# Global attention in a hybrid attention / recurrence / ConvFFN layer: second scores keys-first, values and ones stationary, probabilities streaming

## The chip, the cores and the metric

The kernel runs on one core of one Trainium2 chip. The metric is device time in microseconds (us) of one execution; the time of a kernel is the median of its runs. A core has the engines that the profile calls PE (TensorE, matrix products; PEld is its loading of the stationary operand), DVE (VectorE), ACT (ScalarE), POOL (GpSimd) and SP (SyncE, which here issues the DMAs). Each works through its own list of instructions in order and waits for others by semaphores. In a matrix product one operand is stationary (up to 128 x 128) and the other streams through it column by column into a bank of PSUM; a tile in SBUF or PSUM has 128 partitions.

## What is computed

One layer on 1024 latent tokens of width 1024 and 256 context tokens: a modulated RMSNorm, a projection, three mixers, a gated merge, and a ConvFFN. The change touches the second mixer, `yb`, attention over 1280 keys, 256 of the context and 1024 latent ones, with 8 query heads that share 2 key/value heads of 64 channels:

```python
def dense_attn(q, k, v, sink=None):
    ...
    s = jnp.einsum('bqkgd,bjkd->bkgqj', q.reshape(B_, Lq, KV, G, hd), k).astype(jnp.float32) * hd ** -0.5
    p = jax.nn.softmax(s, axis=-1)[..., :k.shape[1]].astype(v.dtype)
    return jnp.einsum('bkgqj,bjkd->bqkgd', p, v).reshape(B_, Lq, HQ * hd)

def global_attn(q, k, v, ck, cv):
    k_all = jnp.concatenate([ck, k], axis=1)
    v_all = jnp.concatenate([cv, v], axis=1)
    ...

...
ya = window_attn(aq, ak, av, cak, cav, sink_a[l])
yb = global_attn(bq, bk, bv, cbk, cbv)
x_mix = x + m_lat[:, :, 2] * merge_branches(ya, yb, yc, gates, w_branch[l], w_out[l])
```

`dense_attn` is called for each block of 128 queries. In `merge_branches` each mixer's output is lifted to width 1024, multiplied by its sigmoid gate (a part of the projection), summed, and multiplied by `w_out`.

## The kernel before

**Numbers in two halves.** Inputs are fp32. For most products a number is split into a high half, which is the number rounded to fp32r (a cast on ACT), and a low half, which is what remains (a subtraction on DVE). A product is then three matmuls: high by high, high by low, low by high (L190 to L211). Weights come as 512 KB loads `wr` and are split into `wh` and `wl` in `w_unit` (L175, L176). Ordinary transposes on PE are products with an identity matrix, `ident` in fp32 or `identr` in fp32r.

**Stages.** The program computes norms and projections, then the recurrence, then the token-major parts of the projection (L597), then the two attentions in a loop over `br` (L629: 0 is the window attention, 1 the global one), then the merge (L1453) and the ConvFFN. Queries, keys and values lie in DRAM between stages (`q_d`, `kv_d`), and so do the gates (`gate_d`) and the mixers' outputs (`y_d`).

**Order of the work.** The tile framework puts the instructions of each engine into one fixed order when the kernel is built, close to the order in which the program names them, with some priorities (L1322). `weave` (L1214) interleaves generators by their step counts: in each attention the scores of iteration `it + 1`, the values of iteration `it`, and a filler, the products of the gates (`gate_unit` L507: 24 matmuls into one bank for half a unit, tile `gz`, then a copy `gs` on ACT and a store). The window attention has 7 units of gates as filler and the global one 7; 32 filler steps are woven into the lead of each, `FILL0`. PSUM has three tags: `mm`, two tiles of two banks; `a`, two banks; `b`, two banks. A tile of a tag waits until the tile that held its bank is read.

**Global attention.** 16 iterations: 8 blocks of 128 queries, for each of 2 key/value heads (`g`), with its 4 query heads. The lead loads keys and values in five pieces of 256 keys (`prep`, L1247): a load `kv` in a buffer of tag `qf`, `VHL` with the high and low half of the values side by side, 64 columns each, the high halves of the keys twice and the low halves twice (`kk`), their fp32r transposes `kt` in bank `a`, and copies into `KH` and `KL`, which hold 64 channels twice on 128 partitions. The queries (`qprep`, L1273) are split into high and low, which share the 128 partitions of `QT`, so that one product with `KH` gives high times (high and low), and one with `KL` adds low times both.

The scores (`softmax_global`, L1411) are query-first: a tile has 128 queries on the partitions and keys in the columns, 256 context keys of the four heads in `sbc`, 1024 keys of one head in `sbl`, each by a product with `KH` and one with `KL`. DVE takes the largest of each row, ACT the exponential with that bias and the row's sum in the same instruction (`pc`, `plat`); the reciprocals are spread by POOL (L1446) and turned on PE (`pr`, L1314).

The values (L1297) need the keys on the partitions: for each of 10 key tiles, four fp32 transposes turn the probabilities of the four heads into `pp` (L1319, bank `a`), ACT casts the high half `ph` (L1323), DVE subtracts the low half `pl` (L1324), and two tiles later (`PV_LAG`) two products add them into `po` (L1305, L1306, bank `b`), with `VHL` stationary and the 512 columns of 4 heads by 128 queries streaming. At the end the two halves of `po` are added, multiplied by the turned reciprocals, and stored (L1335 to L1342).

## Time and profile before

| | us |
|---|---|
| median of 3 runs (range) | 2117.54 (2116.04 to 2120.67) |
| the profiled execution, its own time | 2119.41 |
| its span, from the first to the last instruction | 2117.6 |

The span by stage, from the view of the profile that sums busy time by windows (us):

| window | stage | PE | DVE | ACT | POOL |
|---|---|---|---|---|---|
| 0 to 700 | norms, projections, recurrence | 680.71 | 413.17 | 206.39 | 57.27 |
| 700 to 880 | window attention | 175.68 | 145.09 | 139.75 | 49.83 |
| 880 to 1210 | global attention | 326.95 | 255.40 | 267.85 | 6.44 |
| 1210 to 1300 | begin of the merge | 89.87 | 49.60 | 31.86 | 0.00 |
| 1300 to 2117 | merge, ConvFFN | 805.13 | 516.14 | 357.12 | 176.14 |

How such a profile is read: the page gives each engine's busy time, the span in forty slices with tenths of busy time in each, and groups of instructions by line with count, busy time, the mean duration of one and the idle time of the engine ahead of them with what ended it. `out<-in` are the program's tile names. The trace gives the same by windows of time and as a timeline of single instructions. A matmul's duration runs from its start to a modelled end; matmuls overlap, so that the pace of PE is read from the distance between starts. In a window's row the engines stand as busy us with the count of instructions, then the clock granted to PE as a share of full speed, the share of the DMA engines, and GB/s. In a timeline's row, `SPq` is the queue of SP, whose instructions issue DMAs.

### The profile page before, as it was taken

What the parts mean: (1) busy time and instruction counts of PE and PEld (TensorE: products, weight loads), DVE (VectorE), ACT (ScalarE), POOL (GpSimd) and SP (SyncE); (2) the same over time, 40 slices, a digit from 0 to 9 for tenths busy, and PEclk for the clock granted to TensorE, in tenths of its full rate; (3) what the DMA queues carried; (4) which work ended last, traced back from release to release, by engine and by line L of the source; (5) the groups of instructions that cost most, each with busy time, mean ns of one, the idle gap of its engine ahead of it and who ended that gap; (6) DMA issues with size and microseconds to landing.
All of it is one profiled execution on the core that took longest, in us unless ns stands there. A gap on an engine that the chain in (4) does not pass through costs nothing.

```text
span 2117.6 us, 30402 instructions
## 1 busy us (share of the span) xinstructions
PE 2078.3 (98%) x11622; PEld 1735.2 (82%) x11622; DVE 1379.4 (65%) x2299; ACT 1003.0 (47%) x1760; POOL 289.7 (14%) x257
## 2 busy tenths in 40 slices
PE   7999999999999999999999999999999999999997
PEld 4888888888988788888888788888888888888887
DVE  4736756636565788677887747569777777664423
ACT  4333323311122877688888734346444444453322
POOL 0000000010022222100000000011333344100111
PEclk9999999999999999999999999999999999999999
DMA  9511111136644221211110454541322222295332
GB/s 364 205 44 36 46 50 32 50 113 201 195 139 134 85 60 53 81 45 33 36 33 28 133 188 147 192 151 49 100 86 84 90 71 89 80 304 192 108 124 85
DMA packets 95489, 229.66 MB, mean 108 GB/s; under 512 B 10736, under 2 KB 35696, under 8 KB 94320
## 3 DMA queue, kind: packets, MB, share of 16 engines
q1 hardware_dynamic: 95344, 227.72, 32.4%
q8 instruction: 91, 1.49, 0.3%
q14 instruction: 54, 0.44, 0.1%
HBM read 182.07 MB, written 45.61 MB: 108 GB/s over the span
## 4 chain that ended last, share of the span: by engine, by line
PE 69%; DVE 3%; ACT 2%; issue 1%; POOL 1%; DMA 1%; DVEq 0%; ACTq 0%; POOLq 0%; SPq 0%
PE pp L1319 5%; PE gz L199 3%; PE gz L200 3%; PE gz L201 3%; PE dn L929 3%; PE dn L930 3%; PE dn L928 3%; PE up L852 2%; PE up L853 2%; PE up L854 2%; PE po L1305 2%; PE po L1306 2%; PE br L200 2%; PE br L201 2%; PE br L199 2%; PE upc L854 2%
## 5 line engine op out<-in xcount | busy, mean ns | idle before, releaser
L175 ACT CAST wh<-wr 128x1024 fp32r<-128x1024 f32 (+1 forms) x139 | 145.1, 1045 | 397.7 <-PE dn L929 71.8
L176 DVE TENSOR_TENSOR wl<-wr,wh 128x1024 fp32r<-128x1024 f32 (+1 forms) x139 | 171.2, 1232 | 226.5 <-ACT wh L175 217.4
L1324 DVE TENSOR_TENSOR pl<-pp,ph 128x512 fp32r<-128x512 f32 x236 | 159.5, 688 | 30.4 <-ACT ph L1323 25.0
L199 PE MATMUL gz<-hh,wh 128*128 128x512 f32 x384 | 156.7, 409 | 2.8 <-ACT gs L523 2.8
L200 PE MATMUL gz<-hl,wh 128*128 128x512 f32 x384 | 152.8, 398 | 0.0
L201 PE MATMUL gz<-hh,wl 128*128 128x512 f32 x384 | 152.6, 398 | 0.0
L1323 ACT CAST ph<-pp 128x512 fp32r<-128x512 f32 x236 | 135.7, 585 | 33.6 <-PE pp L1319 31.1
L210 PE MATMUL tm<-wl,hh 128*128 128x256 f32 x384 | 109.0, 284 | 3.4 <-DVE wl L176 3.4
L211 PE MATMUL tm<-wh,hl 128*128 128x256 f32 x384 | 108.8, 283 | 0.0
L209 PE MATMUL tm<-wh,hh 128*128 128x256 f32 x384 | 108.8, 283 | 0.0
L1305 PE MATMUL po<-ph,VHL 128*128 128x512 f32 x236 | 106.4, 451 | 1.7 <-ACT ph L1323 1.1
L929 PE MATMUL dn<-ac,wh 128*128 128x512 f32 x256 | 99.7, 390 | 0.0
L930 PE MATMUL dn<-ac,wl 128*128 128x512 f32 x256 | 99.6, 389 | 0.0
L928 PE MATMUL dn<-ac,wh 128*128 128x512 f32 x256 | 99.6, 390 | 0.0
L1306 PE MATMUL po<-pl,VHL 128*128 128x512 f32 x236 | 98.0, 415 | 0.1
L199 PEld LDWEIGHTS gz<-hh,wh 128*128 128x128 f32 x384 | 73.0, 190 | 16.5 <-ACT gs L523 5.0
L201 PEld LDWEIGHTS gz<-hh,wl 128*128 128x128 f32 x384 | 72.9, 190 | 15.2
L200 PEld LDWEIGHTS gz<-hl,wh 128*128 128x128 f32 x384 | 73.2, 191 | 11.5
L210 PEld LDWEIGHTS tm<-wl,hh 128*128 128x128 f32 x384 | 73.7, 192 | 4.4 <-DVE wl L176 4.0
L1319 PE MATMUL pp<-ident,plat 128*128 128x128 f32 x512 | 77.1, 274 | 0.0
L1319 PEld LDWEIGHTS pp<-ident,plat 128*128 128x128 f32 x512 | 63.2, 141 | 17.0 <-DVE pl L1324 1.2
L733 ACT ACTIVATE u<-c,cw 128x1024 f32<-128x1024 f32 x38 | 47.3, 1246 | 61.9 <-DVE c L889 33.1
(1402 smaller groups left out, 5899.8 us busy)
## 6 DMA issues: line engine op xcount, KB each, us to landing
wr<-in_w_cm SPq DMA_DIRECT2D x48, 512.0 KB, 3.7
wr<-in_w_up SPq DMA_DIRECT2D x44, 512.0 KB, 3.6
wr<-in_w_down SPq DMA_DIRECT2D x33, 512.0 KB, 3.6
wmr<-in_w_mod SPq DMA_DIRECT2D x32, 512.0 KB, 4.6
gate_d<-gs SPq DMA_DIRECT2D x48, 256.0 KB, 2.0
sgt<-gate_d SPq DMA_DIRECT2D x24, 512.0 KB, 3.3
act_d<-u SPq DMA_DIRECT2D x22, 512.0 KB, 2.6
st<-act_d SPq DMA_DIRECT2D x44, 256.0 KB, 4.2
```

Of the source, the lines that this page charges most:

```text
L175: A.copy(hi[:, :n], raw[:, :n])
L176: (lo_eng or V).tensor_tensor(out=lo[:, :n], in0=raw[:, :n], in1=hi[:, :n].bitcast(F32), op=ALU.subtract)
L199: T.matmul(psl, wh[:, k, c], hh[:, k0 + k, cols], start=s, stop=False)
L200: T.matmul(psl, wh[:, k, c], hl[:, k0 + k, cols], start=False, stop=False)
L201: T.matmul(psl, wl[:, k, c], hh[:, k0 + k, cols], start=False, stop=e)
L210: T.matmul(psl, hh[:, k, toks], wl[:, k % 4, :], start=False, stop=False)
L928: T.matmul(z, w[0][:, c], h[0], start=s, stop=False)
L929: T.matmul(z, w[0][:, c], h[1], start=False, stop=False)
L930: T.matmul(z, w[1][:, c], h[0], start=False, stop=e)
L1305: T.matmul(po, vv, ph, start=n == 0, stop=False)
L1319: T.transpose(pp[:, h], PT(h, n), ident)
L1324: V.tensor_tensor(out=pl, in0=pp, in1=ph.bitcast(F32), op=ALU.subtract)
```

## The change

Only the global attention changes, `attention_t` for `br` 1; the window attention keeps `attention`, with the branches for the global one taken out.

- *Stationary values.* `VV[0]` holds for each key tile and head pair high values, 64 columns of ones, high values; `VV[1]` low values, zeros, low values. Of a stationary block of 128 columns, half is values and half ones (or zeros), so that one product gives the values' sum in 64 rows of `po` and the probabilities' sum in the other 64.
- *Maxima first* (`maxima`). The query-first scores are made with `KH` alone. DVE takes the largest of each row; its negative is written in high and low halves into two columns of `QM`, beside the high half of the queries (which POOL copies there), and turned into `M`.
- *Keys-first scores* (`values`). For each pair of key tiles, four products: `KH` stationary with the turned queries `Q`, and `KL`, which has two rows of ones now, with `M`, so that low keys times high queries and the negative maximum are added in one. ACT takes the exponential `e` of 128 keys by 1024 columns. The cast `ph` is on ACT for even pairs and on POOL for odd ones, the subtraction `pl` on DVE. Three products for each key tile go into `po`, one pair later (`PT_LAG`): high values by `ph`, low values by `ph`, high values by `pl`.
- *Sums last.* ACT copies `po` to `ys`. In the next iteration four products of one row by one column turn the sums (`pr`), DVE takes reciprocals, four fp32 products spread them over the rows (`pb`), and a multiplication and a store end it.
- *Filler and loads.* The gate products of `br` 1 use a bank of tag `a` with one `gs` buffer; the key loads have a tag of their own, `kv`, with one buffer; the casts' buffers are `PT_BUF` = 3.

PE has 9551 rows in the build order before and 9230 after. The diff, cut:

```diff
-                if mode == "b":
-                    z = bank("b", f"gz{n}{i}{hf}", (P, 512))
+                if mode in "ab":
+                    z = bank(mode, f"gz{n}{i}{hf}", (P, 512))
...
-                gs = pool.tile([P, 512], F32, tag="gs", name=f"gs{n}{i}{hf}", bufs=2)
+                gs = pool.tile([P, 512], F32, tag="gs", name=f"gs{n}{i}{hf}", bufs=1 if mode == "a" else 2)
...
-                gen = gate_units(ap_, units, "b")
-                attention(tc, nc, ap_, br, ins, kv_d[br], q_d[br], y_d, mm2, bank, ident, identr, gen, nf)
+                gen = gate_units(ap_, units, "ba"[br])
+                if br == 0:
+                    attention(tc, nc, ap_, br, ins, kv_d[br], q_d[br], y_d, mm2, bank, ident, identr, gen, nf)
+                else:
+                    attention_t(tc, nc, ap_, br, kv_d[br], q_d[br], y_d, mm2, bank, ident, identr, gen, nf)
...
-def softmax_global(nc, tl, mm2, g, nm, QT, KH, KL, res, rs):
...
+def attention_t(tc, nc, ap_, br, kv_d, q_d, y_d, mm2, bank, ident, identr, fill_gen, fill_steps):
...
+    VV = [tl([P, NK, 3, HD], f"VV{j}", 0, 1, F32R) for j in range(2)]
...
+    for v, c in zip(VV, (one, zero)):
+        G.tensor_copy(v[:, :, 1], c[:, None, :].to_broadcast([P, NK, HD]))
+    QM = [tl([P, 4, 2 * HD], f"QM{j}", 0, 1, F32R) for j in range(2)]
+    for q in QM:
+        G.tensor_copy(q[:, :, HD:], zero[:, None, :].to_broadcast([P, 4, HD]))
+    def prep(k0):
+        kv = tl([P, 2, 256], "kv", f"{k0}", 1)
+        SP.dma_start(kv, kv_d[k0:k0 + 2].rearrange("k p n -> p k n"))
...
+        A.copy(vh, vx)
+        V.tensor_tensor(out=vl, in0=vx, in1=vh.bitcast(F32), op=ALU.subtract)
+        kh = tl([P, 2, 2, 2, HD], "kk", f"h{k0}", dt=F32R)
...
+        kl = tl([P, 2, 2, 2, HD], "kk", f"l{k0}", dt=F32R)
+        V.tensor_tensor(out=kl[:, :, :, 0], in0=kx, in1=kh[:, :, :, 0].bitcast(F32), op=ALU.subtract)
+        G.tensor_copy(kl[:, :, :, 1], pad[:, None, None, :].to_broadcast([P, 2, 2, HD]))
+        for kk, dst, nm in ((kh, KH, "h"), (kl, KL, "l")):
+            pt = bank("a", f"kt{br}{k0}{nm}", (P, 2, 2, P), F32R)
+            for k in range(2):
+                for g in range(2):
+                    T.transpose(pt[:, g, k], kk[:, k, g].rearrange("p a b -> p (a b)"), identr)
+            A.copy(dst[:, :, k0 * P:(k0 + 2) * P].rearrange("p g (k c) -> p g k c", k=2), pt)
+    def turn(src, nm):
+        pq = bank("a", f"pq{br}{nm}", (P, 4, P), F32R)
+        for h in range(4):
+            T.transpose(pq[:, h], src[:, h], identr)
+        dst = tl([P, 4, P], nm[0], nm[1:], 3 if nm[0] == "Q" else 2, F32R)
+        A.copy(dst, pq)
+        return dst
+    Q1, Q2 = {}, {}
+    def qprep(it):
+        tt, g = divmod(it, 2)
+        qf = tl([P, 4, HD], "qf", f"q{it}")
+        SP.dma_start(qf, q_d[tt][:, g * 256:(g + 1) * 256])
+        qs = tl([P, 4, 2, HD], "qs", f"q{it}", dt=F32R)
+        A.activation(qs[:, :, 0], qf, AF.Copy, scale=QSCALE)
+        V.scalar_tensor_tensor(out=qs[:, :, 1], in0=qf, scalar=QSCALE, in1=qs[:, :, 0].bitcast(F32),
+                               op0=ALU.mult, op1=ALU.subtract)
+        G.tensor_copy(QM[it % 2][:, :, :HD], qs[:, :, 0].bitcast(F32))
+        Q1[it] = turn(qs.rearrange("p h a b -> p h (a b)"), f"Q{it}")
+    def maxima(it):
+        tt, g = divmod(it, 2)
+        st = tl([P, 5, 4], "st", f"{it}")
+        sc = mm2(f"sbc{it}").rearrange("p a (b c) -> p (a b) c", b=2)
+        for h in range(4):
+            T.matmul(sc[:, h], Q1[it][:, h], KH[:, g, :256], start=True, stop=True)
+        V.tensor_reduce(out=st[:, 0], in_=sc, axis=AX.X, op=ALU.max, negate=True)
+        yield
+        for h in range(4):
+            s2 = mm2(f"sbl{it}{h}")
+            for hf in range(2):
+                k = 256 + hf * 512
+                T.matmul(s2[:, hf], Q1[it][:, h], KH[:, g, k:k + 512], start=True, stop=True)
+            V.tensor_reduce(out=st[:, 1, h:h + 1], in_=s2.rearrange("p a b -> p (a b)"), axis=AX.X, op=ALU.max,
+                            negate=True)
+            if h < 3:
+                yield
+        m = st[:, 2]
+        V.tensor_tensor(out=m, in0=st[:, 0], in1=st[:, 1], op=ALU.min)
+        qm = QM[it % 2]
+        V.tensor_copy(qm[:, :, HD], m)
+        V.tensor_tensor(out=qm[:, :, HD + 1], in0=m, in1=qm[:, :, HD].bitcast(F32), op=ALU.subtract)
+        Q2[it] = turn(qm, f"M{it}")
+        yield
+    def values(it):
+        tt, g = divmod(it, 2)
+        q1, q2 = (q.pop(it).rearrange("p h c -> p (h c)") for q in (Q1, Q2))
+        po = bank("b", f"po{it}", (P, 4, P))
+        def pv(n, ph, pl):
+            for j in range(2):
+                k = 2 * n + j
+                vh, vl = (v[:, k, g:g + 2].rearrange("p a b -> p (a b)") for v in VV)
+                T.matmul(po, vh, ph[:, j], start=k == 0, stop=False)
+                T.matmul(po, vl, ph[:, j], start=False, stop=False)
+                T.matmul(po, vh, pl[:, j], start=False, stop=k == NK - 1)
+        prev = []
+        for n in range(NK // 2):
+            s2 = mm2(f"st{it}{n}")
+            for j in range(2):
+                c = slice((2 * n + j) * P, (2 * n + j + 1) * P)
+                T.matmul(s2[:, j], KH[:, g, c], q1, start=True, stop=False)
+                T.matmul(s2[:, j], KL[:, g, c], q2, start=False, stop=True)
+            ph = tl([P, 2, 512], "ph", f"{it}{n}", PT_BUF, F32R)
+            pl = tl([P, 2, 512], "pl", f"{it}{n}", PT_BUF, F32R)
+            e = tl([P, 2, 512], "e", f"{it}{n}")
+            A.activation(e, s2, AF.Exp)
+            if n % 2:
+                G.tensor_copy(ph, e)
+            else:
+                A.copy(ph, e)
+            V.tensor_tensor(out=pl, in0=e, in1=ph.bitcast(F32), op=ALU.subtract)
+            prev.append((n, ph, pl))
+            if len(prev) > PT_LAG:
+                pv(*prev.pop(0))
             yield
-    V.tensor_tensor(out=r, in0=sm[:, 0], in1=sm[:, 1], op=ALU.add)
-    V.reciprocal(r, r)
-    rb = tl([P, 4, 64], "yT", f"r{nm}")
-    G.tensor_copy(rb, r[:, :, None].to_broadcast([P, 4, 64]))
-    rs[it] = rb.rearrange("p a b -> p (a b)")
-    res[it] = ((lambda h, n: pc[:, h, n * P:(n + 1) * P] if n < 2 else Pl[h][:, (n - 2) * P:(n - 1) * P]),
-               list(range(10)))
-    yield
+        for e in prev:
+            pv(*e)
+        y0, s0 = g * HD, (1 - g) * HD
+        rows = slice(y0, y0 + HD)
+        ys = tl([P, 4, P], "ys", f"{it}")
+        A.copy(ys, po)
+        def sums():
+            pr = bank("a", f"pr{it}", (P, 4, 1))
+            for h in range(4):
+                T.matmul(pr[:, h], ys[s0:s0 + 1, h], one[s0:s0 + 1, 0:1], start=True, stop=True)
+            r = tl([P, 4], "r", f"{it}")
+            V.reciprocal(r, pr.rearrange("p a b -> p (a b)"))
+            def out():
+                pb = bank("a", f"pb{it}", (P, 4, P))[rows]
+                for h in range(4):
+                    T.matmul(pb[:, h], r[:, h:h + 1].to_broadcast([P, HD]), ident, start=True, stop=True)
+                yT = tl([P, 4, P], "yT", f"{it}")[rows]
+                V.tensor_tensor(out=yT, in0=ys[rows], in1=pb, op=ALU.mult)
+                SP.dma_start(y_d[br].rearrange("k (r p) t -> p (k r) t", r=2)[:, 4 * g:4 * g + 4, tt * P:(tt + 1) * P], yT)
+            late.append(out)
+        late.append(sums)
+        yield
+    late = []
+    def lead():
+        for k0 in range(0, NK, 2):
+            prep(k0)
+            yield
+        qprep(0)
+        qprep(1)
+        yield
+        yield from maxima(0)
+    n_it = 2 * LT
+    weave((lead(), 11), (some(fill_gen, FILL0), FILL0))
+    fill_steps -= FILL0
+    for it in range(n_it):
+        if it + 2 < n_it:
+            qprep(it + 2)
+        a, b = (min(fill_steps, int(fill_steps * i / (n_it - SKEW[br]))) for i in (it, it + 1))
+        def main():
+            for j, _ in enumerate(values(it)):
+                if late and j in (1, 2):
+                    late.pop(0)()
+                yield
+        weave((maxima(it + 1), 6) if it + 1 < n_it else (None, 0), (main(), NK // 2 + 1), (some(fill_gen, b - a), b - a))
+    while late:
+        late.pop(0)()
```

What stands on PE where the window attention ends. `po` and `pp` belong to its last iteration, `gz` are gate products, `kt` the transposed keys of the global attention. Before:

```order
L1305 MATMUL po_8473<-ph_158_8497,VHL_0_5970 128x512
L199 MATMUL gz_8560<-hh,wh_8556 128x512
L1306 MATMUL po_8473<-pl_158_8498,VHL_0_5970 128x512
L1305 MATMUL po_8473<-ph_159_8508,VHL_0_5970 128x512
L200 MATMUL gz_8560<-hl,wh_8556 128x512
L1306 MATMUL po_8473<-pl_159_8509,VHL_0_5970 128x512
L201 MATMUL gz_8560<-hh,wl_8557 128x512
```

After (the line numbers here are those of the changed program: L1306 and L1307 are the window attention's value products, L1443 the keys, L201 to L203 the gates):

```order
L1307 MATMUL po_8473<-pl_158_8498,VHL_0_5970 128x512
L1306 MATMUL po_8473<-ph_159_8508,VHL_0_5970 128x512
L1307 MATMUL po_8473<-pl_159_8509,VHL_0_5970 128x512
L1443 MATMUL kt10h<-identr,kk_h_8550 128x128 x4
L1443 MATMUL kt10l<-identr,kk_l_8553 128x128 x4
L201 MATMUL gz_8574<-hh,wh_8570 128x512
L202 MATMUL gz_8574<-hl,wh_8570 128x512
L203 MATMUL gz_8574<-hh,wl_8571 128x512
```

Before, gate products start among the last value products, and 33 of them precede the first keys on PE; after, the two keys' transposes of the first piece follow the last value product, and all gate products stand behind them.

What stands on PE inside an iteration. Before, `pp` are transposes of the probabilities of one key tile, `po` value products and `sbl` scores of the next iteration:

```order
L201 MATMUL gz_10170<-hh,wl_10167 128x512
L1319 MATMUL pp_10420<-ident,plat_7_0_10190 128x128
L1319 MATMUL pp_10420<-ident,plat_7_1_10230 128x128
L1319 MATMUL pp_10420<-ident,plat_7_2_10254 128x128
L1319 MATMUL pp_10420<-ident,plat_7_3_10286 128x128
L1305 MATMUL po_10369<-ph_71_10387,VHL_0_8531 128x512
L1306 MATMUL po_10369<-pl_71_10388,VHL_0_8531 128x512
L1431 MATMUL sbl_1_10431<-KH_0_8529,QT_8_10139 128x512
L1432 MATMUL sbl_1_10431<-KL_0_8530,QT_8_10139 128x512
```

After, `sbl` are the scores for the maxima, `st` the keys-first scores (`VV_0_8531` are the high values with ones, `VV_0_8532` the low ones with zeros):

```order
L1503 MATMUL po_9015<-ph_10_9021,VV_0_8531 128x512
L1504 MATMUL po_9015<-ph_10_9021,VV_0_8532 128x512
L1505 MATMUL po_9015<-pl_10_9022,VV_0_8531 128x512
L1481 MATMUL sbl_9061<-KH_0_8529,Q_2_8850 128x512
L1503 MATMUL po_9015<-ph_11_9035,VV_0_8531 128x512
L1512 MATMUL st_9065<-Q_1_8736,KH_0_8529 128x512
L1513 MATMUL st_9065<-M_1_8965,KL_0_8530 128x512
```

The groups of four transposes are gone from here; three value products stand for each key tile where two stood, and a keys-first pair of scores beside the query-first one.

On ACT, the exponentials and casts of one iteration after the change:

```order
L1517 ACTIVATE e_100_10550<-st_10543 128x1024
L1521 CAST ph_100_10548<-e_100_10550 128x1024
L1517 ACTIVATE e_101_10564<-st_10557 128x1024
L1517 ACTIVATE e_102_10599<-st_10592 128x1024
L1521 CAST ph_102_10597<-e_102_10599 128x1024
```

The casts of `e_101` and of `e_103` stand on POOL's queue (L1519) and not on ACT's.

65 lines of the change are left out of this document (22 added, 43 removed).

## The prediction

> **What bounds the kernel now.** I read the page's first parts, then the windows of the global attention, then TensorE's timeline inside one iteration, and last the timelines of the place where the window attention ends. The first rows are from the page: busy time by engine, and PE in forty slices.
>
> ```profile
> PE 2078.3 (98%) x11622; PEld 1735.2 (82%) x11622; DVE 1379.4 (65%) x2299; ACT 1003.0 (47%) x1760; POOL 289.7 (14%) x257
> PE   7999999999999999999999999999999999999997
> ```
>
> PE is busy 98% of the span, without a hole from end to end. The changed stage is the second attention. Its first scores start at about 900 us and its last values at 1208 us; the windows in it (busy us of PE, PEld, DVE, ACT, POOL, then the granted clock) read:
>
> ```profile
> 900.00:1000.00 100.00, 99.66 (x573) 80.97 (x572) 80.40 (x134) 83.20 (x181) 2.01 (x5) 1.00 0.13 42
> 1000.00:1100.00 100.00, 99.31 (x581) 82.24 (x580) 80.37 (x136) 82.49 (x178) 2.42 (x6) 1.00 0.10 32
> ```
>
> Two things are to be seen. PE sets the pace in this stage; ACT and DVE, at 80 to 83%, are close behind but not the limit. So ACT and DVE work that goes away is worth only the waits it causes on PE, and PE work is paid in full. What a PE instruction costs is not its duration (they overlap) but the distance to the next start. A piece of PE's timeline (start, duration, line, tiles, count):
>
> ```profile
> 1002.65 0.29 PE L1284 MATMUL pq<-identr,qs_q 128*128 128x128 f32 x2
> 1002.78 0.47 PE L1306 MATMUL po<-pl,VHL 128*128 128x512 f32 x1
> 1003.08 0.29 PE L1284 MATMUL pq<-identr,qs_q 128*128 128x128 f32 x2
> ...
> 1003.51 0.28 PE L1421 MATMUL sbc__9929<-KH,QT 128*128 128x256 f32 x1
> 1003.63 0.28 PE L1422 MATMUL sbc__9929<-KL,QT 128*128 128x256 f32 x1
> 1003.75 0.60 PE L1319 MATMUL pp<-ident,pc__9716 128*128 128x128 f32 x4
> 1004.11 0.47 PE L199 MATMUL gz<-hh,wh 128*128 128x512 f32 x1
> 1004.42 0.39 PE L200 MATMUL gz<-hl,wh 128*128 128x512 f32 x1
> 1004.64 0.39 PE L201 MATMUL gz<-hh,wl 128*128 128x512 f32 x1
> 1004.88 0.60 PE L1319 MATMUL pp<-ident,pc__9716 128*128 128x128 f32 x4
> 1005.23 0.48 PE L1431 MATMUL sbl<-KH,QT 128*128 128x512 f32 x1
> 1005.54 0.39 PE L1432 MATMUL sbl<-KL,QT 128*128 128x512 f32 x1
> 1005.77 0.40 PE L1431 MATMUL sbl<-KH,QT 128*128 128x512 f32 x1
> ...
> 1007.38 0.68 PE L1314 MATMUL pr<-ident,yT_r__9861 128*128 128x128 f32 x4 [0.29 <-DVE pl L1324]
> 1007.82 0.48 PE L1305 MATMUL po<-ph,VHL 128*128 128x512 f32 x1
> ```
>
> The prices: a 512-column matmul 0.23 us (1005.54 to 1005.77), a 256-column one 0.12. Four fp32 transposes take 0.36 (1003.75 to 1004.11), and the matmul behind them holds PE 0.31 instead of 0.23, so a group costs **0.44**. Four fp32r transposes are twice 0.13 plus about 0.07 behind them, **0.33**. The two fp32 products of `pr` stand as four records, 0.11 each: 0.44, and 0.08 behind them.
>
> **The change, part by part.** The counts of before are in these groups (busy us, mean ns, idle before):
>
> ```profile
> L1319 PE MATMUL pp<-ident,plat 128*128 128x128 f32 x512 | 77.1, 274 | 0.0
> L1305 PE MATMUL po<-ph,VHL 128*128 128x512 f32 x159 | 72.7, 457 | 0.7 <-ACT ph L1323 0.3 <-DVE yT L1339 0.2
> L1432 PE MATMUL sbl<-KL,QT 128*128 128x512 f32 x128 | 50.5, 395 | 0.0
> L1323 ACT CAST ph<-pp 128x512 fp32r<-128x512 f32 x160 | 91.8, 588 | 19.3 <-PE pp L1319 17.6
> L1324 DVE TENSOR_TENSOR pl<-pp,ph 128x512 fp32r<-128x512 f32 x160 | 107.7, 688 | 22.7 <-ACT ph L1323 17.8
> ```
>
> Removed on PE, for each of the 16 iterations: the KL half of the query-first scores, 8 x 0.23 = 1.84 and 4 x 0.12 = 0.48; 40 transposes (32 of `plat`, 8 of `pc`) in ten groups, 10 x 0.44 = 4.40; `pr`, 0.52; the 20 old value products, 4.60. That is **11.84 us**.
>
> Added: the keys-first scores, 10 key tiles x 2 x 0.23 = 4.60; the value products, 10 x 3 x 0.23 = 6.90, because half of each stationary block is now ones (or zeros) and the low part of V needs a product of its own; the turning of the maxima (`M`), 0.33. Then two operations that no row shows. The four sums (one row by one column, fp32) would be eight records after the pattern of `pr`: between the pace of fp32r transposes, 8 x 0.06 = 0.5, and that of `pr`, 8 x 0.11 = 0.88; with the 0.08 behind them I take 0.75. If four records do, 0.26 is the lower end. The four broadcasts `pb` have 128 fp32 columns like `pr`, eight records of 0.11 and 0.08 behind, 0.96; the lower end is a transpose group, 0.44. The sum is **13.54 us**, 1.7 more than what goes, and 16 x 1.7 = **27 us** longer on the engine that bounds the stage. With both unknowns at their lower ends it is 1.0 less each time, 16 us less in all.
>
> Off PE the change relieves. ACT loses ten casts of 0.59, one copy of 1.0, the four 256-wide exponentials and the two copies of `po`; it gains one more 1024-wide exponential (1.12), three wide casts and two copies: some 17 us of each iteration become 11 to 12. DVE's five subtractions at the 1.23 that a 128x1024 subtraction from SBUF takes (the page's group of L176) are 6.2 against 10 x 0.69, with the five reductions unchanged. None of that shortens PE's list. I cost it at the waits it can remove: 16 x (11.84 + 2.65 kept) + 279 gate products x 0.23 + 19 of the merge x 0.23 is 300 of the 307 us between 900 and 1207, so at most 7 us are waits, most of it in the last iteration, whose length still hangs on exponentials, casts and subtractions. I take **-2**.
>
> **Where the stage begins** a wait is added. The gate products `gz` move from bank `b` to bank `a`, where the transposed keys `kt` are claimed first. Before, 33 gate products stand on PE between the last `po` and the first `kt`; after, none. What they covered:
>
> ```profile
> 878.22 0.39 PE L1306 MATMUL po<-pl,VHL 128*128 128x512 f32 x1
> 878.45 0.39 PE L201 MATMUL gz<-hh,wl 128*128 128x512 f32 x1
> ...
> 885.73 0.39 PE L200 MATMUL gz<-hl,wh 128*128 128x512 f32 x1
> 885.96 0.47 PE L1268 MATMUL kt<-identr,qs_kk 128*128 128x128 f32 x4
> 880.78 0.96 SPq L1249 DMA_DIRECT2D qf_kv<-kv_d  x2
> 883.57 0.41 ACT L1253 CAST VHL<-qf_kv 128x256 fp32r<-128x256 f32 x1
> 884.19 0.40 ACT L1259 CAST qs_kk<-qf_kv 128x256 fp32r<-128x256 f32 x1
> qf_kv<-kv_d SPq DMA_DIRECT2D x5, 256.0 KB, 2.8
> ```
>
> The first key load is issued at 880.78, behind the last store on SP's queue; it lands, and the last cast of it ends at 884.6. From 878.2 to then PE now stands, **6.4 us**; the gate products are done later at their full price. Everything behind `kt` on PE's queue waits with it. Next, `kv` has one buffer where the old loads had two: each of the four later loads waits until the one before is read, 0.4 to issue, 2.8 to land and about 1.1 to read, 17 us for four, while PE holds 48 gate products and ten groups of keys between the first and last of them, 14 us. That is 2 to 3 more. The clock may also be cut by the idle time, as it was after a gap near the end of this stage:
>
> ```profile
> 1190.00:1192.00 2.00, 1.09 (x6) 0.53 (x4) 1.66 (x2) 1.96 (x5) 0.00 (x0) 1.00 0.91 295
> 1192.00:1194.00 2.00, 1.68 (x7) 1.53 (x8) 1.96 (x5) 1.10 (x2) 0.00 (x0) 0.61 0.99 342
> 1194.00:1196.00 2.00, 2.00 (x8) 1.71 (x7) 1.79 (x3) 1.28 (x3) 0.00 (x0) 0.54 0.96 371
> ```
>
> About 3.4 us near half clock lose 1.7, part of it under the wait for keys. I take **+9** for the beginning, between 4 (the loads run ahead) and 14.
>
> POOL has two new casts of 128x1024 in each iteration, and here a price must be bounded:
>
> ```profile
> L581 POOL COPY tbA<-cs x2: 611/612/612, 466.2 to 466.8; 128x512 f32<-128x512 f32 x2
> L1137 POOL COPY S<-S x8: 614/1501/1512, 180.6 to 415.0; 64x512 f32<-64x512 f32 x8
> L887 POOL TENSOR_TENSOR c<-c,c x19: 1289/2270/2286, 1506.2 to 1848.3; 128x512 f32<-128x512 f32 x19
> ```
>
> A 512-wide copy takes 0.61, or 1.50 in most of the cases of L1137. So a 1024-wide cast is 1.1 at best and 2.0 at the same added 0.9. The odd tile's probabilities come that much later; while it is 1.1, the order leaves room (between the scores of tile 1 and its first value product stand some 3.5 us of other PE work, against 1.12 for the exponential and 1.1 for the cast). I take 1.1, and nothing on PE, and keep 0.9 twice in each iteration as the upper end. The Trainium skill, GPSIMD Engine Reference, section Key points, says that GpSimd shares its SBUF interfaces with VectorE and contends with VectorE instructions that have two SBUF inputs. That speaks against this change, whose new subtraction reads both inputs from SBUF where the old one read `pp` from PSUM; the two durations of L887 and of L1137 look like it. By that rule the sum would be that of the second rival below.
>
> **The sum.** 27 + 9 - 2 = 34 us on the profiled execution's own 2119.4 (span 2117.6), 2153.4. That execution is 1.9 above the median of the runs shown, so I forecast 2152.
>
> **The rivals.**
> *The loop waits as well*: POOL's casts, and the subtractions beside them, take the long form and the slack of the order is gone. Half of 2 x 0.9 in each iteration is +14, all of it +29: 2166 to 2181. For it: DVE is still some 70% busy and alternates reductions and subtractions, so lateness is passed on. Against: the even tile's subtraction runs while ACT makes the odd exponential, before POOL starts.
> *Only the count of PE*: the keys come earlier than I think (+4) and relieved ACT takes nearly all waits away (-7): +24, 2142; with the cheap sums and broadcasts as low as 2133. For it: the drop from 17 to 12 us on ACT. Against: SP's order puts the key load behind the same last store as before.
> *Not slower*: the value products stream closer than 0.23, three in a row into one bank with no transposes between them. There are 480 of them, so from 34 / 480 = 0.07 less, at 0.16 each, the change is even; at the 0.12 of a 256-column product it is 53 faster than forecast, 2099. Against it: every 512-column interval above is 0.22 or more, among them three in a row into one bank (`gz`). The Trainium skill, TensorE: Matmul & The Clock Gate, section Back-to-back issue gap, gives about 131 ns for a 512-column matmul in a sustained stream with weight loads; by that the change would be faster, and the rows here, at 0.23, do not agree.
>
> **How the numbers follow.** Forecast 0.58, loop waits 0.23, only the count 0.13, not slower 0.06. The range reaches from the low end of the third case to the high end of the second, 2133 to 2181; outside it are the last case and few others. A measurement of this kernel tells about 0.2% (4 us) from no change; only the last case reaches that or less: faster 0.04, same 0.02, slower 0.94.
>
> **What would show it.** In the changed profile: 480 value products at 0.23 from start to start, and about 16.2 us of PE in each iteration without gates; PE idle for some 6 us where the window attention ends, released by the cast of the keys, with a clock below 1 behind it; ACT below 65% in the windows of the stage. POOL casts with two durations, and PE waiting for `ph` of odd tiles, mean the second case. I am wrong if value products stand closer than 0.16, or if PE's part of an iteration is below 14.5 us.

## The result, and the profile after

The changed kernel takes 2167.02 us (median of 4 runs, 2165.75 to 2169.69); the kernel before, beside it, 2117.62 (2116.04 to 2120.67). The ratio is 1.0226 with a 95% interval of 1.0213 to 1.0239: slower by 49 us. The span of the profiled execution goes from 2117.6 to 2164.7, +47.1.

From the page of the changed kernel, busy time by engine and PE in forty slices:

```profile
PE 2117.6 (98%) x11526; PEld 1756.2 (81%) x11526; DVE 1357.1 (63%) x2154; ACT 933.5 (43%) x1442; POOL 342.3 (16%) x298
PE   7999999999999999899999999999999999999997
```

PE's busy time grows by 39.3 us, its idle time by 7.8, in a dip at one slice, where the global attention begins. The windows of the loop (busy us of PE, PEld, DVE, ACT, POOL, then the granted clock):

```profile
900.00:1000.00 100.00, 98.29 (x476) 77.74 (x476) 63.61 (x76) 49.10 (x62) 15.32 (x13) 1.00 0.13 41
1000.00:1100.00 100.00, 99.91 (x487) 78.99 (x485) 63.68 (x76) 51.11 (x61) 17.75 (x15) 1.00 0.09 27
```

ACT falls from 83 to 51%, DVE from 80 to 64%, and PE stays full: the work that left was not the work that bounds the stage. The costliest groups of the new loop:

```profile
L1503 PE MATMUL po<-ph,VV 128*128 128x512 f32 x160 | 65.4, 409 | 1.4 <-ACT ph L1521 1.0
L1505 PE MATMUL po<-pl,VV 128*128 128x512 f32 x160 | 63.3, 396 | 1.2 <-DVE pl L1522 1.2
L1522 DVE TENSOR_TENSOR pl<-e,ph 128x1024 fp32r<-128x1024 f32 x80 | 97.1, 1218 | 29.8 <-ACT ph L1521 26.3
```

PE waits 1.0 us for casts and 1.2 for subtractions in the whole stage (the last numbers of the first two rows; more of it is hidden, see `M` below). Of POOL's casts, the view of that line has the shortest, the median and the longest:

```profile
L1519 POOL CAST ph<-e x32: 1041/1044/2018, 923.5 to 1245.8; 128x1024 fp32r<-128x1024 f32 x32
```

24 take 1.04 us and 8 take 1.17 to 2.02. Each of the 8 begins while one of DVE's subtractions is running, and none of the 24 overlaps one. The subtraction keeps its 1.20 to 1.23; the cast, which begins later, is the one that becomes longer:

```profile
1005.06 1.20 DVE L1522 TENSOR_TENSOR pl<-e,ph 128x1024 fp32r<-128x1024 f32 x1
1005.49 1.67 POOL L1519 CAST ph<-e 128x1024 fp32r<-128x1024 f32 x1 [4.86 <-ACT e L1517]
```

Then PE's timeline around the operations that no row of before showed: the sums `pr`, the spreading `pb`, the turning of the maxima `M`, and, ahead of them, the cast on ACT for which the product behind `M` waits.

```profile
1018.59 1.05 ACT L1521 CAST ph<-e 128x1024 fp32r<-128x1024 f32 x1
1019.19 0.54 PE L1449 MATMUL pq1M<-identr,QM 128*128 128x128 f32 x4
1019.69 0.50 PE L1503 MATMUL po<-ph,VV 128*128 128x512 f32 x1
...
1045.69 0.39 PE L1513 MATMUL st<-M,KL 128*128 128x512 f32 x1
1046.01 1.05 PE L1537 MATMUL pr<-one,ys 1*128 1x1 f32 x8
1046.98 0.73 PE L1481 MATMUL sbl<-KH,Q 128*128 128x512 f32 x2
1047.56 0.39 PE L201 MATMUL gz<-hh,wh 128*128 128x512 f32 x1
...
1061.85 0.54 PE L1449 MATMUL pq1M<-identr,QM 128*128 128x128 f32 x4
1062.23 0.50 PE L1503 MATMUL po<-ph,VV 128*128 128x512 f32 x1
1062.56 0.39 PE L1504 MATMUL po<-ph,VV 128*128 128x512 f32 x1
...
1219.46 0.39 PE L1505 MATMUL po<-pl,VV 128*128 128x512 f32 x1
1219.78 1.09 PE L1544 MATMUL pb<-ident,r 128*64 128x128 f32 x8
1220.80 0.50 PE L202 MATMUL gz<-hl,wh 128*128 128x512 f32 x1
1221.13 0.40 PE L203 MATMUL gz<-hh,wl 128*128 128x512 f32 x1
```

Three things are to be seen. A 512-column product still holds PE 0.23 us, alone or three in a row into one bank. The product *ahead* of `pr` and of `pb` holds it 0.32. And the groups hold it longer than their 8 x 0.11: `pr` costs 1.29 - 0.23 ahead of the pair and 0.12 in it, **1.18**; `pb` 1.34 - 0.23 and 0.10 behind, **1.21**; `M` 0.38 and 0.10, **0.48**. Over all 16 iterations the means are 1.18 for `pr`, 1.30 for `pb`, which stands in 20 pieces, and 0.61 for `M`: the group at 1061.85 is the cheapest of its kind. In the 15 iterations in which a value product follows `M`, that product starts 0.05 us after ACT's cast of its `ph` ends (1018.59 + 1.05 and 1019.69 above). So about 0.13 of the 0.61 is a wait for the cast, which the trace books mostly as the length of `M`'s last record and not as idle time.

Where the stage begins, the windows (columns as above) and PE's waits between 870 and 1270:

```profile
874.00:876.00 2.00, 2.00 (x10) 1.85 (x9) 0.83 (x2) 1.12 (x2) 0.00 (x0) 0.57 0.78 214
876.00:878.00 2.00, 1.91 (x5) 0.99 (x3) 0.69 (x1) 0.11 (x2) 0.00 (x0) 0.58 0.42 163
878.00:884.00 6.00, 0.06 (x1) 0.07 (x1) 1.85 (x8) 1.81 (x6) 2.41 (x5) 0.76 0.40 109
884.00:886.00 2.00, 1.83 (x10) 1.55 (x11) 1.02 (x3) 1.61 (x4) 1.53 (x3) 0.50 0.31 102
886.00:888.00 2.00, 2.00 (x6) 1.59 (x5) 0.79 (x2) 1.02 (x3) 0.00 (x0) 0.52 0.52 164
```

```profile
PE kt10h L1443 <- ACT kk_h L1435: 6.0, 1, 6.0
...
PE pp L1312 <- DVE pl L1317: 1.0, 1, 1.0
...
PE pq1Q L1449 <- ACT KL L1444: 0.9, 1, 0.9
PE po L1306 <- ACT ph L1316: 0.8, 1, 0.8
```

PE stands 6.0 us for the first keys, and 0.8 and 1.0 already in the tail of the window attention, where no gate product fills the wait for its last subtraction (the 0.8, for a cast, is there with the gate products too). Behind each of the two the granted clock is near half, for some 4 us of busy time each in this execution.

### The profile page after: what moved, and what is told of

Same layout as the page of the kernel before. It is cut to its first block, busy times and chain, and to the rows that moved or that the text cites. A ratio compares the mean times of both kernels' runs of the same rounds, so it can differ in the third digit from the quotient of the medians.

```text
span 2164.7 us, 29677 instructions
## 1 busy us (share of the span) xinstructions
PE 2117.6 (98%) x11526; PEld 1756.2 (81%) x11526; DVE 1357.1 (63%) x2154; ACT 933.5 (43%) x1442; POOL 342.3 (16%) x298
## 4 chain that ended last, share of the span: by engine, by line
PE 71%; DVE 2%; ACT 2%; POOL 1%; issue 1%; DMA 1%; DVEq 0%; POOLq 0%; ACTq 0%; SPq 0%
PE gz L201 3%; PE gz L202 3%; PE gz L203 3%; PE dn L934 3%; PE dn L933 3%; PE dn L935 3%; PE up L857 2%; PE up L858 2%; PE up L859 2%; PE br L202 2%; PE br L201 2%; PE br L203 2%; PE po L1503 2%; PE st L1512 2%; PE st L1513 2%; PE upd L858 2%
## 5 line engine op out<-in xcount | busy, mean ns | idle before, releaser
L201 PE MATMUL gz<-hh,wh 128*128 128x512 f32 x384 | 156.3, 407 | 3.7 <-ACT gs L525 3.3
L203 PE MATMUL gz<-hh,wl 128*128 128x512 f32 x384 | 151.5, 395 | 0.0
L1517 ACT ACTIVATE e<-st 128x1024 f32<-128x1024 f32 x80 | 81.9, 1026 | 133.7 <-PE st L1513 127.4
L1522 DVE TENSOR_TENSOR pl<-e,ph 128x1024 fp32r<-128x1024 f32 x80 | 97.1, 1218 | 29.8 <-ACT ph L1521 26.3
L1482 DVE TENSOR_REDUCE st<-sbl 128x1 f32<-128x1024 f32 x64 | 78.1, 1221 | 43.6 <-PE sbl L1481 43.6
L201 PEld LDWEIGHTS gz<-hh,wh 128*128 128x128 f32 x384 | 73.1, 190 | 19.7 <-ACT gs L525 5.3
L203 PEld LDWEIGHTS gz<-hh,wl 128*128 128x128 f32 x384 | 72.8, 190 | 15.5
L202 PE MATMUL br<-yl,wh 128*128 128x512 f32 x192 | 74.8, 390 | 0.0
L203 PE MATMUL br<-yh,wl 128*128 128x512 f32 x192 | 74.5, 390 | 0.0
L201 PE MATMUL br<-yh,wh 128*128 128x512 f32 x192 | 74.5, 390 | 0.0
L211 PEld LDWEIGHTS tm<-wh,hh 128*128 128x128 f32 x384 | 73.7, 192 | 0.8 <-ACT qo L617 0.4
```

The lines of the kernel that those rows point to most:

```text
L201: T.matmul(psl, wh[:, k, c], hh[:, k0 + k, cols], start=s, stop=False)
L202: T.matmul(psl, wh[:, k, c], hl[:, k0 + k, cols], start=False, stop=False)
L203: T.matmul(psl, wl[:, k, c], hh[:, k0 + k, cols], start=False, stop=e)
L211: T.matmul(psl, hh[:, k, toks], wh[:, k % 4, :], start=s, stop=False)
L1522: V.tensor_tensor(out=pl, in0=e, in1=ph.bitcast(F32), op=ALU.subtract)
```

## The experiments

Theories: **A**, the loop is PE's list, and the sums, the spreading and `M` are dearer than forecast; **B**, the loop waits for POOL's casts and the subtractions beside them (the second case of the prediction, whose times hold the measured one). For the begin: the gate products' place, or the key loads. Runs are compared through their ratio to the kernel before, timed on the same chip; 0.001 is 2.1 us, and a difference of two ratios is known to about 0.002. The spans of single profiled executions differ by up to 4 us already ahead of the window attention, so where a trace is asked for a time, it is counted from that stage's first score (`sa`) to the first product of the ConvFFN (`up`): 725.1 us before (700.3 to 1425.4), 772.9 after (700.0 to 1472.9), +47.8. In the table, "less than after" is the difference to 1.0226 in us.

| run | median us | ratio (95%) | less than after |
|---|---|---|---|
| e1_no_pr | 2151.08 | 1.0163 (1.0146 to 1.0180) | 13 |
| e2_no_pr_pb | 2132.66 | 1.0078 (1.0063 to 1.0093) | 31 |
| e3_act_casts | 2163.00 | 1.0225 (1.0210 to 1.0240) | 0 |
| e4_gate_b | 2154.80 | 1.0184 (1.0169 to 1.0199) | 9 |
| b1_pp_twice (on before) | 2182.35 | 1.0308 (1.0292 to 1.0323) | |
| e5_no_vl | 2135.92 | 1.0089 (1.0072 to 1.0106) | 29 |
| f1_shift | 2168.82 | 1.0245 (1.0230 to 1.0260) | -4 |
| f2_shift_b | 2157.12 | 1.0192 (1.0176 to 1.0207) | 7 |
| f3_pool_sum | 2206.47 | 1.0420 (1.0403 to 1.0437) | -41 |
| e6_full_tile | 2157.64 | 1.0189 (1.0173 to 1.0205) | 8 |
| f4_full_b_act | 2146.74 | 1.0138 (1.0122 to 1.0154) | 19 |
| f5_full_b_no_vl | 2120.24 | 1.0014 (1.0005 to 1.0023) | 45 |

**The sums and the spreading.** e1_no_pr takes the reciprocals of ones:

```diff
-            pr = bank("a", f"pr{it}", (P, 4, 1))
-            for h in range(4):
-                T.matmul(pr[:, h], ys[s0:s0 + 1, h], one[s0:s0 + 1, 0:1], start=True, stop=True)
...
-            V.reciprocal(r, pr.rearrange("p a b -> p (a b)"))
+            V.reciprocal(r, one[:, 0:4])
```

> The four one-column products of the sums (pr) are left out, and the reciprocals are taken of ones, so the output is not divided by its sum; all else stays. Theory A (the turning of the sums and its spreading are dearer on PE than forecast): the trace of the changed kernel has 1.06 us from the product ahead of pr to the one behind it beyond a product's own 0.23, and 0.13 in the pair behind, 1.19 in each iteration, so -19 us: 2148. The forecast's price of 0.75 would give -12: 2155, its lower end of 0.26 -4: 2163. Theory B (the 15 us above the forecast are waits of the loop on POOL's casts and the subtractions beside them): PE's list is not what ends it, so about 0 to -5: 2162 to 2167.

e2_no_pr_pb leaves `pb` out as well:

```diff
-                pb = bank("a", f"pb{it}", (P, 4, P))[rows]
-                for h in range(4):
-                    T.matmul(pb[:, h], r[:, h:h + 1].to_broadcast([P, HD]), ident, start=True, stop=True)
...
-                V.tensor_tensor(out=yT, in0=ys[rows], in1=pb, op=ALU.mult)
+                V.tensor_tensor(out=yT, in0=ys[rows], in1=ys[rows], op=ALU.mult)
```

> As the run without pr, and the four fp32 products that spread the reciprocals (pb) are left out too; DVE multiplies ys with itself instead, so the output is not normalised. Theory A: pb stands in the changed kernel's trace at 1.2 us where its eight records are together and at 1.57 where they are in two pieces, some 1.35 in each iteration; with pr 2.55 x 16 = -41 us: 2126. The forecast's prices, 0.75 and 0.96, would give -27: 2140. Theory B: 0 to -8: 2159 to 2167.

13 and 31 us less: PE's list is what counts, and B is wrong by far. A expected 19 and 41. In the trace of e1 `pb` stands in 29 pieces instead of 20 and takes 1.51 in each iteration instead of 1.30, 3.4 us in all; 16 x 1.18 less that is 15.5, and from `sa` to `up` 15.8 are gone. With both out, PE's waits for subtractions grow from 1.2 to 3.7 us; the rest of what is missing to 41 was not taken apart. The two together are worth 1.96 us per iteration by the medians and 2.03 from `sa` to `up` (772.9 to 740.4); the forecast had 1.71.

**The casts.** All on ACT:

```diff
-            if n % 2:
-                G.tensor_copy(ph, e)
-            else:
-                A.copy(ph, e)
+            A.copy(ph, e)
```

> All five casts of the probabilities on ACT, none on POOL. Theory A: POOL's casts cost nothing on PE, which stands at 99.8% in the windows of the loop; ACT goes from 52% to some 62% and has room: 2167, within 3. Theory B: the casts on POOL and the contention with the subtractions were the lateness, so -14 to -29 goes: 2138 to 2153.

No difference. The subtraction's mean is 1218 ns with the casts on POOL and 1218 without:

```profile
L1519 DVE TENSOR_TENSOR pl<-e,ph 128x1024 fp32r<-128x1024 f32 x78 | 94.7, 1218 | 26.0 <-ACT ph L1518 25.6
```

Where casts and subtractions meet in the changed kernel it is the cast that gives way, and taking it off POOL gains nothing. So B falls, though the measured time lies where it said.

**The begin.** The gate products in tag `b` again (with one `gs` buffer, as in the change):

```diff
-                gen = gate_units(ap_, units, "ba"[br])
+                gen = gate_units(ap_, units, "bB"[br])
...
-                if mode in "ab":
-                    z = bank(mode, f"gz{n}{i}{hf}", (P, 512))
+                if mode in "abB":
+                    z = bank(mode.lower(), f"gz{n}{i}{hf}", (P, 512))
```

> The gate products of the global attention go back to PSUM tag b (still one gs buffer); all else as changed. Theory A: they stand on PE ahead of the first keys again and cover the load of the keys: 6.0 us idle before the first keys, 1.8 in the tail of the window attention, and two stretches near half clock (874 to 877.5 and 884 to 888, some 3.5 lost, of which one may come back at another gap): -8 to -11 us, 2156 to 2159. Rival C (the single-buffered load chain of the keys sets the begin, whatever covers it): -4 or less, 2163 to 2167. If the two tiles of tag b are now short, because po holds one for a whole iteration, waits of gz on gs appear in the loop and it gains less.

9 us less by the medians and 9.3 from `sa` to `up` (763.6). Two of the windows above, in this run:

```profile
876.00:878.00 2.00, 2.00 (x10) 1.66 (x9) 0.00 (x0) 0.48 (x1) 1.64 (x4) 1.00 0.79 226
878.00:884.00 6.00, 6.00 (x33) 5.02 (x32) 2.68 (x6) 4.08 (x12) 1.85 (x3) 1.00 0.45 135
```

PE is full and the clock is whole. The single key buffer stays in this run, and PE waits only 1.0 us for keys in all: it was the cover that was missing, not the loads that became slow.

**What the change removes.** The kernel before, with each group of transposes issued twice:

```diff
-            for h in range(4):
+            for h in [0, 1, 2, 3] * (1 + br):
                 T.transpose(pp[:, h], PT(h, n), ident)
```

> The kernel before, with the four fp32 transposes of each key tile of the global attention issued twice (the second time over the first result). It tests the price of what the change removes. By the forecast four transposes hold PE 0.36 us, and the 0.08 on the matmul behind a group is paid once in any case: 160 x 0.36 = +58 us, 2175. If PE had room there (its 98% were slack), the transposes would be nearly free: 2117 to 2130. If they cost more than their intervals say (casts and subtractions late, since the second set delays the read of pp), 2190 or more.

+65 us where 58 were expected, 0.41 for each of 160 groups. The expectation paid the short last record of a group (0.03 where the others take 0.11) twice, and it comes once: in this run's trace a doubled group stands 0.79 ahead of the product behind it where a single one stands 0.36. Four more transposes are four times 0.11, which is the 0.44 at which the forecast had a group go. This bears out the transposes, 4.40 of the 11.84; the other terms of the removed side were not tried by themselves.

**The third value product.**

```diff
-                T.matmul(po, vl, ph[:, j], start=False, stop=False)
```

> The changed kernel without the products of the low values (L1504), so the low part of V is left out of the output. 160 products go. Theory A: each is worth its interval of 0.228 us: -36 us, 2131, less some 3 of new waits on the subtractions, as in the run without sums and broadcasts: 2131 to 2134. If value products can stream closer where nothing else is in the way, the two that are left per tile show intervals below 0.22 in the trace. Theory B (the loop is held by ACT, DVE and POOL): a gain of 15 or less, 2152 or more.

29 us, by the medians and from `sa` to `up` (743.7); 36 less some 3 were expected. No value product stands closer than 0.22 behind another; the median distance from one value product to the next start, between 930 and 1170 us, is 0.231 where it was 0.227, and `pb` stands in 33 pieces and takes 1.60 in each iteration, 4.8 us more in all. B is refuted again.

**Two other ways to the reciprocals.** f1_shift takes them from the 64 copies of the sum; f2_shift_b does the same with the gates in tag `b`:

```diff
+            yT = tl([P, 4, P], "yT", f"{it}")[rows]
+            A.copy(yT, ys[s0:s0 + HD])
+            V.reciprocal(yT, yT)
+            V.tensor_tensor(out=yT, in0=ys[rows], in1=yT, op=ALU.mult)
```

> The changed kernel with another end: the 64 rows of ones already give the sum 64 times over, so ACT copies these 64 rows of ys to the other 64 partitions, DVE takes their reciprocals (64x512) and multiplies; the products pr and pb go. Theory A: what they cost on PE goes as in the run that left both out, with 15.3 and 19.5 us less span: 2130 to 2136, if one more ACT copy and a long reciprocal on DVE are hidden. DVE is 64% busy, and a reciprocal of up to 3 us in each iteration of 21 would still fit; if it is longer, or delays the subtractions that stand behind it, the gain is given back: 2140 to 2155.

> Both: the sums' rows copied by ACT, and the gate products in tag b. Theory A: the two gains add up, -32 and -10 to -12: 2120 to 2126, about as the kernel before. If tag b is short (po is held until ys is copied, and gz wants the other tile), less: 2130.

Both missed: nothing is gained. From the trace of f1_shift, a group of DVE and two of PE's waits:

```profile
L1537 DVE RECIPROCAL yT<-yT 64x512 f32<-64x512 f32 x14 | 46.9, 3347 | 27.9 <-ACT yT L1536 27.9
```

```profile
PE po L1505 <- DVE pl L1522: 11.6, 22, 1.1
PE po L1503 <- ACT ph L1521: 5.0, 7, 2.4
```

A reciprocal of 64 rows and 512 columns takes 3.35 us; the subtraction behind it is late, and PE's waits in the loop sum to some 24 us where they were some 3. That is part of what PE was spared; the rest was not taken apart. In nine cases, too, a cast of POOL begins ahead of a subtraction here, and then it is the subtraction that becomes longer:

```profile
1046.73 1.04 POOL L1519 CAST ph<-e 128x1024 fp32r<-128x1024 f32 x1 [4.75 <-ACT e L1517]
1046.74 2.11 DVE L1522 TENSOR_TENSOR pl<-e,ph 128x1024 fp32r<-128x1024 f32 x1
```

f3_pool_sum lets POOL add the exponentials, so that two products per key tile do, with values packed as before the change (the diff shows the main lines; the casts are all on ACT, `e` has a third buffer, and the sums come one step later):

```diff
+                vv = VHL[:, k, g].rearrange("p a b -> p (a b)")
+                T.matmul(po, vv, ph[:, j], start=k == 0, stop=False)
+                T.matmul(po, vv, pl[:, j], start=False, stop=k == NK - 1)
...
+                G.tensor_tensor(out=a2, in0=acc, in1=e, op=ALU.add)
...
+        G.tensor_tensor(out=asum.rearrange("p a b -> p (a b)"), in0=acc[:, 0], in1=acc[:, 1], op=ALU.add)
```

> The sums are taken off the value products: the stationary block is high and low values side by side, as before the change, so that two products per key tile do (the third was 2.28 us of PE in each iteration); POOL adds the five exponentials (four additions of 128x1024, one of 128x512), four fp32 products turn the sum as pr did, POOL spreads the reciprocals over 64 columns and two fp32 products turn them back (0.6 in place of 1.2). The casts are all on ACT, the gate products in tag b. Theory A (what PE has to do sets the time): from the run with the gates in tag b, 2155, 16 x (2.28 + 0.6) = -46: 2109, with up to 5 of new waits 2114; this would be faster than the kernel before. Theory B (the other engines are near their limit): POOL needs 4 x 2.6 + 1.3 = 12 us in each iteration by the 1.29 of a 512-wide addition, in an iteration of 18; if its additions take the long form, 2.29 for 512 columns, it is 20 us and POOL sets the pace: 2140 or more.

41 us more than the change instead of 58 less. Two groups of DVE, one of POOL and two waits of PE from its trace:

```profile
L1516 DVE TENSOR_TENSOR pl<-e,ph 128x1024 fp32r<-128x1024 f32 x80 | 159.2, 2001 | 29.7 <-ACT ph L1515 29.3
L1480 DVE TENSOR_REDUCE st<-sbl 128x1 f32<-128x1024 f32 x64 | 77.5, 1218 | 13.1 <-PE sbl L1479 12.7
```

```profile
L1521 POOL TENSOR_TENSOR acc<-acc,e 128x1024 f32<-128x1024 f32 x48 | 122.3, 2549 | 72.7 <-ACT e L1514 69.0
```

```profile
PE po L1502 <- DVE pl L1516: 25.4, 27, 1.7
PE pb L1553 <- POOL rb L1547: 21.8, 13, 2.6
```

Beside POOL's additions DVE's subtractions, which read two tiles of SBUF, go from 1.22 to 2.00 us in the mean; its reductions, which read PSUM, stay at 1.22. POOL's additions alone would fit, as the better case of the expectation had it (2.55 each); it is the subtractions and the copy `rb` behind the additions that PE waits for, and the granted clock falls to 0.96 between 930 and 1260 us. How much each of these costs was not taken apart. The Trainium skill, GPSIMD Engine Reference, section Key points, names such a contention with VectorE instructions of two SBUF inputs; this run agrees with it. So do the changed kernel and f1_shift, whose POOL casts read one tile only: there the instruction that begins second is the longer one, be it POOL's cast (8 of 32 in the changed kernel) or DVE's subtraction (nine in f1_shift).

**The shape of the stationary block.** The extra 0.09 ahead of `pr` and `pb` and their long tails are not there at the old `pr`, which is fp32 too. What differs is the block: 1x128 and 128x64 instead of 128x128. e6_full_tile makes both full; the surplus rows of `pb` are not read, and `sel` is a column of the identity that picks the row of the sum:

```diff
-                T.matmul(pr[:, h], ys[s0:s0 + 1, h], one[s0:s0 + 1, 0:1], start=True, stop=True)
+                T.matmul(pr[:, h], ys[:, h], sel[:, g:g + 1], start=True, stop=True)
...
-                pb = bank("a", f"pb{it}", (P, 4, P))[rows]
+                pb = bank("a", f"pb{it}", (P, 4, P))
...
-                    T.matmul(pb[:, h], r[:, h:h + 1].to_broadcast([P, HD]), ident, start=True, stop=True)
+                    T.matmul(pb[:, h], r[:, h:h + 1].to_broadcast([P, P]), ident, start=True, stop=True)
```

> The changed kernel with the same sums and broadcasts on full stationary blocks of 128x128: pr has the whole of ys (128 rows) stationary and streams a column that picks the one row, pb has each reciprocal spread over 128 columns in place of 64. Theory D (the array pays for a change of the stationary block's shape): in the trace of the changed kernel the product ahead of a group of pb or pr is 0.32 instead of 0.23 long from start to start, the group's last record takes 0.20 or 0.175 and the one behind 0.34; where the kernel before streams 128x128 fp32 blocks (its own pr), nothing is paid ahead, the last record takes 0.03 and the one behind 0.31. So pb goes from 1.21 to 0.88 and pr from 1.18 to 0.9 or less, -0.6 to -1.0 in each of 16 iterations: -10 to -16 us, 2151 to 2157, and 319 becomes 228 to 235 ahead of the groups. Rival E (it is the fp32 weight loads or the entering of a PSUM bank that costs, whatever the block's shape): 2165 to 2169, and the intervals stay.

8 us less, and the intervals of ratio do not meet those of the change. PE's timeline in this run:

```profile
1044.04 0.39 PE L1516 MATMUL st<-M,KL 128*128 128x512 f32 x1
1044.27 0.95 PE L1540 MATMUL pr<-sel,ys 128*128 128x1 f32 x8
1045.08 0.72 PE L1484 MATMUL sbl<-KH,Q 128*128 128x512 f32 x2
1045.64 0.40 PE L201 MATMUL gz<-hh,wh 128*128 128x512 f32 x1
...
1131.55 0.39 PE L1508 MATMUL po<-pl,VV 128*128 128x512 f32 x1
1131.77 1.05 PE L1547 MATMUL pb<-ident,r 128*128 128x128 f32 x8
1132.58 0.48 PE L201 MATMUL gz<-hh,wh 128*128 128x512 f32 x1
```

The product ahead is back at 0.23 and 0.22, the groups take 0.81 instead of 0.97 and 1.02: with what follows, 0.27 and 0.31 less for a group. Over all iterations both now take 0.91, 0.27 and 0.39 less, since `pb` stands in 20 pieces here too. That is 9 to 11 us of 16 iterations, measured 8; most of the -10 to -16 that was expected is too much. The Trainium skill, TensorEngine Tiling (Array Packing), section Key Properties, says that a change of tiling mode drains TensorE. The rows show a price at a change of the block's shape, about 0.3 for a group that goes there and back; that these blocks are tiling modes of their own they do not show.

f4_full_b_act joins the full blocks, the gates in `b` and the casts on ACT.

> The full blocks, the gate products in tag b and all casts on ACT together. Theory D with the run of tag b (2155): -10 to -16, and 0 to -2 for the casts: 2137 to 2145. Rival E: 2153 to 2156. In either case slower than the kernel before: the third value product, 2.28 in each iteration, is still paid.

19 us less than the change, the sum of the parts (8 + 9 + 0, within what is known of each), and still 1.4% above the kernel before. f5_full_b_no_vl leaves out the products of the low values too.

> The full blocks, the gates in tag b, all casts on ACT, and no product of the low values: V enters rounded to its high half, so the low part of V is left out of the output. Theory D (PE's list, group entries included, is the time): without the low values the run before lost only 29 to 31 us in place of 160 x 0.228 = 36, because the spread products pb stood in 33 pieces instead of 20, and each piece costs 0.34 with a 64-column block: 13 x 0.34 = 4.4. With full blocks a piece costs some 0.1, so nearly all of the 36 should come: 2147 - 34 = 2113, between 2109 and 2117, below or at the kernel before. If other waits take over (subtractions late, as where sums and spread products were left out), 2118 to 2122.

It comes out at 1.0014 (1.0005 to 1.0023): 0.1% above the kernel before, in the expectation's second case and not in its first, and that without the low part of V, which the kernel before has for nothing in the second half of its stationary block. 26 us came of the 36 of the 160 products. `pb` stands in 40 pieces now and still takes 0.94 in each iteration, where 20 pieces took 0.91 in e6: with full blocks a piece more costs next to nothing. From the trace:

```profile
1100.00:1200.00 100.00, 95.96 (x471) 75.58 (x470) 71.63 (x82) 70.87 (x79) 2.99 (x3) 1.00 0.19 61
```

PE is no longer full, and its waits for the maxima, casts and subtractions, some 4 us in f4_full_b_act, are some 8. So here the other engines begin to bind; the rest of the missing 10 us was not taken apart. No version that was tried beats the kernel before.

## Why the prediction was right, and where it was too low

*PE bounds the stage and is paid in full.* Right: ACT lost more than a third of its time in the loop and nothing came of it; taking PE work out (e1, e2, e5) shortened the kernel, taking POOL's work out (e3) did not.

*The removed side, 11.84.* Supported for the transposes: 0.41 for four of them by doubling the groups, against 0.44 in the sum. The rest stands on intervals of the trace alone.

*The added side, 13.54.* The products were right in price: 0.227 to 0.228 from start to start, a little below the 0.23 used. The terms without a row were too small, and they are the step of the sum that fell short. In each iteration `pr` takes 1.18 where 0.75 stood, `pb` 1.30 where 0.96 stood, and `M` 0.61 where 0.33 stood, with the wait of 0.13 in it: +1.05, 17 us in all. Their bounds failed too: they came from rows with 128x128 blocks only, whatever their operation, and `pr` and `pb` lie above the highest price that those rows allow, 0.96. With full blocks, in e6, both take 0.91 and are inside it. What is left of `M` was only seen in the trace and not tried by itself. Against them stands the pace: some 75 products of 512 columns in an iteration (58 of its own and 17 of the gates) at 0.003 less each are -4 us. 27 + 17 - 4 is 40 for the loop; the measured 47.8 less the 9.3 of the begin is 38.5. Summed from start to start, PE's part of an iteration without gates goes from 14.8 us to 17.3; the prediction had 14.5 and 16.2.

*The begin, +9.* The size was right (9 by e4's medians, 9.3 from `sa` to `up`), in part by luck. 6.0 idle before the first keys against 6.4 forecast; then a wait of 1.0 in the tail of the window attention, where 0.5 stood before, and a second stretch at half clock there, some 1.7, which were not foreseen; and none of the 2 to 3 that the single key buffer was to cost.

*Waits, -2.* Nothing: PE's waits in the loop sum to 3 us before and 4 after, and some 2 more hide behind `M`.

*The rivals.* "The loop waits as well" gave 2166 to 2181 and the time is 2167.0. One of its signs came, the two durations of POOL's casts, and POOL and DVE do stand in each other's way; but as a price its mechanism is out by e3, where all of that is gone and the time stays: a time inside a case's range is no evidence for the case. "Not slower" fell at its own condition: no interval of value products near 0.16. "Only the count of PE" had the loop about right in kind and too small; its low end, 2133, is not what its terms give, since 2142 less the 16 of the cheap sums and broadcasts is 2126.

## What to carry to other kernels

A change that moves work off busy but waiting engines and adds as much to the one that bounds has to be counted on that engine alone, and there the small products count too: eight records with one row or 64 columns cost as much as five full products of 512 columns. Where a new product's stationary block has another shape than its neighbours, pad it to theirs. Filler work whose bank or buffer is shared with a stage's first loads stops being filler just where it is needed.

## What was not expected of the hardware

- fp32 products with a 1x128 or 128x64 stationary block among 128x128 ones hold the product ahead 0.32 us instead of 0.23, and their last record 0.175 to 0.20; each return costs again, so that nine more pieces of `pb` cost 3.4 us in e1, about 0.37 each. With 128x128 blocks, 20 more pieces cost 0.5 us in all (f5 beside e6).
- DVE's reciprocal goes by columns: 0.16 us for 128x1, 0.20 for 128x8 and 3.35 for 64x512 in f1_shift, 0.0062 to 0.0063 for each column more, at 64 rows as at 128.
- Where one of POOL's casts and one of DVE's subtractions with two inputs in SBUF overlap, the one that begins second becomes longer and the first mostly keeps its time: POOL's cast goes from 1.04 to 1.67 or 2.02 in the changed kernel, DVE's subtraction from 1.22 to 2.11 in f1_shift. So it is in all overlaps of these two runs; in f2_shift_b three casts that begin 0.06 to 0.11 us ahead of a subtraction are the longer ones all the same. DVE's reductions from PSUM stay at 1.22.
- Two short waits of PE, 0.8 and 1.0 us within 3 us, stand at the end of the window attention in seven of the profiles. In five of them (the changed kernel, e1, e2, e3, e5) the clock is near half for 3.4 us right behind them; in e6 and f1 it stays whole there and falls only in the wait of 6 us that follows. With 0.8 and 0.5, as in the kernel before and e4, it stays whole in all of the other seven.
